# Feed-forward rows prepared in steps behind each output tile; the output stage's products in a written order; the last tile's turns behind the first feed-forward products

## The chip, the core and the metric

The kernel runs on one core of one Trainium2 chip. The core has a matrix engine (TensorE, PE in the profile, with its weight loads listed as PEld), a vector engine (VectorE, DVE), a scalar engine (ScalarE, ACT), GpSimd (POOL) and a sync engine (SP) that here only issues transfers. Each engine works through its own queue in order; engines wait for one another by semaphores. The metric is the time of one execution on the device in microseconds; the time before is the median of three runs, 2523.09 us (2523.03 to 2525.29).

## The reference

One layer of a streaming encoder for 2048 prompt rows and 8 sequences of 16 sample rows, 17 tiles of 128 rows with D = 1024 columns. The change touches the output projection with its two norms and the start of the feed-forward part:

```python
    mix = jnp.concatenate([o, sc_out.astype(x.dtype)], axis=-1) @ w_o
    x = x + rmsnorm(mix, norm_mix_post)

    h = rmsnorm(x, norm_ffn_pre)
    f = (jax.nn.silu(h @ w_gate) * (h @ w_up)) @ w_down
    x = x + rmsnorm(f, norm_ffn_post)
```

All of it is float32. The kernel gets that precision from products of split operands: each operand is cast to a short form (`h`, by ACT) and the rest of it is kept as a second operand (`l`, by a subtraction on DVE or POOL), and each product is three matmuls: h with h, h with l, l with h.

## The kernel before

The program runs in stages: the mixer (input projection and the two head groups), the **output stage** (`o_tile`, once for each tile t of 0 to 16), the feed-forward products (`gate_up`, three groups of rows with 22 column blocks each), and the down projection. The first two stages leave what the next one reads in DRAM; the feed-forward input goes through DRAM too (`hTd`, one tensor for each of three groups of tiles, 0 to 5, 6 to 11 and 12 to 16).

**One output tile.** `o_load(t)` has SP load two halves of the mixer's output (`mr`, one buffer) and the residual rows (`xo`, two buffers). `mix_split` makes the split operand of each half: ACT casts to `mh`, DVE subtracts to `ml`; each of the two names has three buffers of half a tile. Then PE makes 48 products of 512 columns, 8 blocks of rows of `w_o` by three split terms by two halves of the output, into two PSUM banks (`dbank`, of three buffers, and `tbank`, of two). Behind them comes a chain over several engines: two squares with a sum on ACT; a small sum on DVE, and the reciprocal root by a DVE and a POOL instruction (`rstd`, names `oxm`, `oxr`); two products with the gains on DVE, which scale in the bank; two additions to `xo`; two squares of `xo` on ACT; another small sum and root (`oym`, `oyr`); and `hx`, the normed rows, 1024 columns in one instruction, on DVE. Then comes what I call the **turn** of the tile: eight transposes on PE into two `ftbank` banks, two multiplications on DVE into `ht`, and a store of `ht` to `hTd` by ACT's queue.

**The weights of the output projection** (`woh` and `wol`, eight blocks of rows) are cast and subtracted in the stage itself. Blocks 0 and 1 come from SBUF. Blocks 2 to 7 come by DMA through the two buffers that `xo` uses later, so the load of a block waits until the block two before it has been split.

**Preparation of the first feed-forward group.** Between `o_tile` 0 to 7 (`O_SPLIT` = 8) and the rest, `ffn_load(0)` loads the eight blocks of rows of `hTd` of group 0 (`fh`). `ffn_sums` makes four differences (`ft3`) and four more in place. `ffn_prep` makes seven split operands (`PARTS`) of four blocks each: an ACT cast to `xh` and a subtraction to `xl`, with one block in four of group 0 on POOL; two of the seven parts need a further subtraction each. One part stands ahead of each of the next seven `o_tile`.

**What sets the order.** A scheduler that fills each engine's queue from its own model of readiness; written order is a priority only. So before, products of neighbouring tiles mix on PE, and the turns stand where the scheduler puts them. `tc.issue_after(x)` keeps what is inside it behind instruction x. `tc.manual_schedule(engines={PE})`, used in the mixer before, makes PE keep the written order.

**The start of the feed-forward products.** `ffetch` has weights loaded, combined and split; `gu_start(0, 0)` makes four products of 12 matmuls each, and `gate_up` three more and what follows on ACT, DVE and POOL. The eight PSUM banks are used in turn, three `dbank`, two `tbank`, three `ftbank`.

Of the kernel before, what the change touches and what calls it, by code (L numbers as in the profile page):

```python
# [1 line left out]

# [15 lines left out]
P = 128  # L18
D = 1024
KD = D // P  # L20
# [3 lines left out]
NT = 17  # L24
# [20 lines left out]
O_SPLIT = 8  # L45
NPD, NPT, NPG = 3, 2, 2
NR, NKV, NACC = 3, 2, 3
XKB = 4
# [4 lines left out]
NWE = 4  # L53
# [31 lines left out]
def kernel(  # L85
# [28 lines left out]
    nc = tc.nc  # L114
    V, A, G, T = nc.vector, nc.scalar, nc.gpsimd, nc.tensor
# [44 lines left out]
    with ExitStack() as ph:  # L160
# [856 lines left out]
            nc.sync.dma_start(out=xt, in_=x[t])  # L1017
            return mr, xt

        ahead = []  # L1020

        def o_tile(t):
            mr, xt = ahead.pop() if ahead else o_load(t)
            pss = [psd.tile([P, 512], F32, tag="d", name="dbank"), tbank()]
            for kh in range(2):
                mh, ml = mix_split(mr[kh]) if t else ready_m[kh]
                for j in range(4):
                    k = 4 * kh + j
                    for ci, (m_, w_) in enumerate(((mh, woh), (mh, wol), (ml, woh))):
                        for n in range(2):  # L1030
                            T.matmul(pss[n], m_[:, j, :], w_[k][:, n * 512:(n + 1) * 512],  # L1031
                                     start=(k == 0 and ci == 0), stop=(k == KD - 1 and ci == 2))
            ss = op.tile([P, 4], F32, tag="oss", name="oss", bufs=2)
            for n in range(2):
                A.activation(ojunk, pss[n], AF.Square, accum_out=ss[:, n:n + 1])
            V.tensor_add(ss[:, 0:1], ss[:, 0:1], ss[:, 1:2])
            r = rstd(op, ss[:, 0:1], 1, 1.0 / D, EPS, "ox")
            for n in range(2):
                c = slice(n * 512, (n + 1) * 512)
                V.scalar_tensor_tensor(pss[n], pss[n], r, gpost[:, c], op0=ALU.mult, op1=ALU.mult)  # L1040
                V.tensor_add(xt[:, c], xt[:, c], pss[n])
            nc.scalar.dma_start(out=x2d[t], in_=xt)
            for n in range(2):
                A.activation(ojunk, xt[:, n * 512:(n + 1) * 512], AF.Square, accum_out=ss[:, 2 + n:3 + n])
# [3 lines left out]
            V.tensor_scalar_mul(hx, xt, r)  # L1048
            ht = op.tile([P, KD, P], F32, tag="ht", name="ht") if t else spare[1]
            for n in range(2):  # L1050
                ps = pft.tile([P, 512], F32, tag="t", name="ftbank")
                for q in range(4):
                    k = 4 * n + q
                    T.transpose(ps[:, q * P:(q + 1) * P], hx[:, k * P:(k + 1) * P], ident)
                V.tensor_mul(ht[:, 4 * n:4 * n + 4, :], ps.rearrange("p (k c) -> p k c", k=4),
                             g_ffn[:, 4 * n:4 * n + 4].unsqueeze(2).broadcast_to([P, 4, P]))
            gi, i = FPLACE[t]
            nc.scalar.dma_start(out=hTd[gi][:, :, i * P:(i + 1) * P], in_=ht)

        for t in range(O_SPLIT):  # L1060
            o_tile(t)
        ahead.append(o_load(O_SPLIT))


    nbank = [0]
# [66 lines left out]
    with ExitStack() as ph:  # L1132
# [9 lines left out]
        def blocks(gi, hs, k):  # L1142
            hw = len(FGROUPS[gi]) * P // 2
            return hs[k][:, :hw], hs[k][:, hw:2 * hw], hs[KH + k][:, :hw], hs[KH + k][:, hw:2 * hw]

        def ffn_sums(gi, hs, fs):
            hw = len(FGROUPS[gi]) * P // 2
            t3, t2 = [], []
            for k in range(KH):
                b11, b12, b21, b22 = blocks(gi, hs, k)  # L1150
                t3.append(fs.tile([P, HW], F32, tag="t3", name="ft3", bufs=KH)[:, :hw])
                V.tensor_sub(t3[k], b22, b12)
                V.tensor_sub(b12, b12, b11)
# [5 lines left out]
            return t3, t2  # L1159

        def ffn_prep(gi, hs, sums):
            hw = len(FGROUPS[gi]) * P // 2
            t3, t2 = sums
            X = {nm: ([], []) for nm in PARTS}
            for nm in PARTS:
                for k in range(KH):
                    b11, b12, b21, b22 = blocks(gi, hs, k)
                    if nm == "T2" and not gi:
                        V.tensor_sub(b12, b22, b12)
                    elif nm == "T4":  # L1170
                        V.tensor_sub(t2[k], b21, t2[k])
# [4 lines left out]
                    (G if k == 0 and not gi else V).tensor_tensor(  # L1176
                        out=l[:, :hw], in0=v, in1=h[:, :hw].bitcast(F32), op=ALU.subtract)
                    X[nm][0].append(h)
                    X[nm][1].append(l)
                yield X  # L1180
# [70 lines left out]
        def gu_start(gi, f, X):  # L1251
            hw = len(FGROUPS[gi]) * P // 2
            g_, f_, W, _ = fpend[0]
            assert (g_, f_) == (gi, f)
            banks = [fbank()[:, :hw] for _ in range(4)]
            for b, w, nm in zip(banks, W, ("B11", "T3", "T1", "T2")):
# [71 lines left out]
        for gi in range(len(FGROUPS)):  # L1328
# [2 lines left out]
            if gi + 1 < len(FGROUPS):  # L1331
                hload, hs = ffn_load(gi + 1, fd), []
            for f in range(NF):
                gate_up(gi, f, hid, gu_start(gi, f, hid))
                if gi + 1 < len(FGROUPS):
                    if 4 <= f < 4 + KD:
                        with tc.issue_after(wl[0].ins):
                            hs.append(next(hload))
                    if f == NF - 6:
                        t3 = ffn_sums(gi + 1, hs, fd)  # L1340
# [233 lines left out]
```

## Time and profile before

| what | value |
|---|---|
| median of three runs | 2523.09 us |
| the profiled execution: time, and span from first to last instruction | 2523.03 us, 2521.2 us |
| DVE, ACT, POOL busy over the span | 1616.9 us (64%), 1059.6 us (42%), 591.8 us (23%) |
| first product of the output stage | at 906.18 us |
| last product of the output stage | at 1114.88 us |
| the two turns behind that | at 1116.67 and 1132.38 us |
| chain that ended last, by engine | PE 77%, DVE 10%, DMA 5%, ACT 3%, issue 3% |

Times in the profile count from the start of the span. A row of the timeline gives start, duration, engine, line and operation, output and inputs, shapes, and in brackets how long the engine had been idle and what ended that. Matmuls overlap: a row of 0.39 us is followed by the next about 0.23 us later.

### The profile page before, as it was taken

The numbers are of one execution on the slowest core, as the hardware profiler recorded it, in microseconds if no ns is written. First come the engines' busy times: TensorE is split into PE (matmuls) and PEld (weight loads), VectorE is DVE, ScalarE is ACT, GpSimd is POOL, SyncE is SP. The second block draws the span as 40 slices with busy tenths as digits, with TensorE's granted clock in tenths as the row PEclk, the third lists the DMA queues.
The fourth block names the chain that finished last, engine by engine and source line by source line (L and its number), as shares of the span: only waits on it lengthen the run. The fifth ranks groups of instructions, "written<-read, shape, count | busy, mean of one in ns | idle before, by whom it ended". The sixth has DMA issues, their size and how long they took to land.

```text
span 2521.2 us, 39375 instructions
## 1 busy us (share of the span) xinstructions
PE 2462.7 (98%) x14366; PEld 2251.4 (89%) x14366; DVE 1616.9 (64%) x3025; ACT 1059.6 (42%) x2355; POOL 591.8 (23%) x663
## 2 busy tenths in 40 slices
PE   8999999999999999999999999999999999999998
PEld 7988888889999988789999999999999987888786
DVE  5966645545666555868878754545555564677698
ACT  5656445445435343534344422223333345333343
POOL 1101011011010001325556400000000045455564
PEclk9999999999999999999999999999999999999999
DMA  7865555556676556668877878878888844343476
GB/s 264 319 209 194 211 193 192 176 181 226 229 239 237 195 187 223 222 229 319 276 262 260 292 245 276 269 247 259 286 275 303 264 142 129 98 124 123 128 225 184
DMA packets 282498, 561.91 MB, mean 223 GB/s; under 512 B 26108, under 2 KB 174784, under 8 KB 265024
## 3 DMA queue, kind: packets, MB, share of 16 engines
q1 hardware_dynamic: 161200, 483.52, 57.2%
q10 hardware_dynamic: 121104, 75.88, 9.7%
q8 instruction: 113, 1.85, 0.3%
q14 instruction: 81, 0.66, 0.1%
HBM read 400.62 MB, written 158.70 MB: 222 GB/s over the span
## 4 chain that ended last, share of the span: by engine, by line
PE 77%; DVE 10%; DMA 5%; ACT 3%; issue 3%; POOL 1%; ACTq 0%; SPq 0%; DVEq 0%; POOLq 0%
PE fbank L1248 31%; PE dbank L298 21%; PE fbank L1406 10%; PE tbank L1031 3%; PE dbank L1031 3%; DVE xr L1424 1%; DVE acc L1365 1%; DVE acc L302 1%; PE gbank L155 1%; PE tbank L343 1%; DMA partd<-pt 1%; DMA xt<-in_x 1%; PE obank L694 1%; PE gbank L749 1%; PE gbank L702 1%
## 5 line engine op out<-in xcount | busy, mean ns | idle before, releaser
L1248 PE MATMUL fbank<-xh,fw 128*128 128x384 f32 (+1 forms) x3696 | 899.5, 326 | 7.9 <-ACT m L1282 3.5
L298 PE MATMUL dbank<-hi,w 128*128 128x384 f32 (+1 forms) x2240 | 673.3, 369 | 9.1 <-ACT w L277 6.3
L1248 PEld LDWEIGHTS fbank<-xh,fw 128*128 128x128 f32 x3696 | 651.9, 188 | 9.8 <-ACT m L1282 4.3
L1248 PE MATMUL fbank<-xl,fw 128*128 128x384 f32 (+1 forms) x1848 | 602.5, 326 | 0.0
L1406 PE MATMUL fbank<-dw,as 128*128 128x512 f32 x1980 | 458.8, 393 | 8.5 <-DVE as L1390 2.5
L298 PEld LDWEIGHTS dbank<-hi,w 128*128 128x128 f32 x2240 | 417.6, 190 | 48.5 <-ACT w L277 6.6
L1406 PEld LDWEIGHTS fbank<-dw,as 128*128 128x128 f32 x1980 | 370.4, 188 | 96.6 <-DVE acc L1365 4.2
L298 PE MATMUL dbank<-lo,w 128*128 128x384 f32 (+1 forms) x1120 | 402.8, 360 | 1.1 <-DVE lo L216 1.1
L1248 PEld LDWEIGHTS fbank<-xl,fw 128*128 128x128 f32 x1848 | 347.4, 188 | 0.0
L1390 POOL TENSOR_TENSOR as<-ar,as 128x256 fp32r<-128x256 f32 (+1 forms) x207 | 187.1, 914 | 276.8 <-ACT as L1387 273.1
L298 PEld LDWEIGHTS dbank<-lo,w 128*128 128x128 f32 x1120 | 213.3, 190 | 18.7 <-DVE lo L216 1.7
L1365 DVE TENSOR_TENSOR acc<-acc,fbank 128x512 f32<-128x512 f32 x248 | 166.2, 682 | 92.8 <-PE fbank L1406 74.8
L1387 ACT CAST as<-ar 128x256 fp32r<-128x256 f32 (+1 forms) x288 | 118.1, 427 | 182.0 <-PE fbank L1406 133.4
L1105 POOL TENSOR_TENSOR dw<-dr,dw 128x512 fp32r<-128x512 f32 x52 | 77.1, 1495 | 484.6 <-ACT dw L1103 484.4
L1223 ACT CAST fw<-rg 128x512 fp32r<-128x512 f32 x124 | 77.4, 624 | 194.6 <-PE fbank L1248 150.0
L302 DVE SCALAR_TENSOR_TENSOR acc<-R,cw,acc 128x384 f32<-128x384 f32 (+2 forms) x180 | 121.7, 678 | 53.1 <-ACT acc L332 44.4
L1295 DVE TENSOR_TENSOR c<-u,fbank 128x384 f32<-128x384 f32 (+1 forms) x66 | 34.9, 528 | 101.1 <-PE fbank L1248 101.1
L1293 ACT ACTIVATE m<-fbank 128x384 f32<-128x384 f32 (+1 forms) x66 | 31.3, 474 | 125.0 <-PE fbank L1248 113.7
L1291 DVE TENSOR_TENSOR m<-m,m 128x384 f32<-128x384 f32 (+1 forms) x44 | 23.1, 526 | 93.3 <-ACT m L1284 93.3
L324 POOL COPY hist<-R 128x3 f32<-128x3 f32 x60 | 18.5, 308 | 255.5 <-ACT R L307 202.0
L1224 POOL TENSOR_TENSOR fw<-rg,fw 128x512 fp32r<-128x512 f32 x44 | 69.7, 1583 | 34.3 <-ACT fw L1223 34.1
L1224 DVE TENSOR_TENSOR fw<-rg,fw 128x512 fp32r<-128x512 f32 x80 | 56.5, 706 | 17.7 <-ACT fw L1223 15.2
(356 smaller groups left out, 3489.3 us busy)
## 6 DMA issues: line engine op xcount, KB each, us to landing
w<-wsplit SPq DMA_DIRECT2D x105, 1024.0 KB, 5.1
fw<-fsplit SPq DMA_DIRECT2D x188, 512.0 KB, 4.7
fsplit<-fw SPq DMA_DIRECT2D x94, 512.0 KB, 4.2
partd<-pt ACTq DMA_DIRECT2D x88, 384.0 KB, 6.9
rg<-in_w_gu SPq DMA_DIRECT2D x62, 512.0 KB, 4.1
wsplit<-w SPq DMA_DIRECT2D x28, 1024.0 KB, 4.9
ar<-partd SPq DMA_DIRECT2D x48, 384.0 KB, 3.2
wr<-in_w_in SPq DMA_DIRECT2D x34, 512.0 KB, 5.9
```

The source lines that it names most:

```text
L298: T.matmul(ps[:, :c], l[:, k, :], r[k][:, :c], start=(k == 0 and r is hi and l is wh), stop=(k == KD - 1 and l is wl))
L302: r = V.scalar_tensor_tensor(acc, raw(d), w[:, d:d + 1], acc, op0=ALU.mult, op1=ALU.add)
L1031: T.matmul(pss[n], m_[:, j, :], w_[k][:, n * 512:(n + 1) * 512], start=(k == 0 and ci == 0), stop=(k == KD - 1 and ci == 2))
L1105: e.tensor_tensor(out=w[:, 1], in0=v, in1=w[:, 0].bitcast(F32), op=ALU.subtract)
L1223: A.copy(w[:, 0], v)
L1224: e.tensor_tensor(out=w[:, 1], in0=v, in1=w[:, 0].bitcast(F32), op=ALU.subtract)
L1248: T.matmul(ps, w_[:, c], b_[k][:, :hw], start=(first and k == 0 and ci == 0), stop=(k == KH - 1 and ci == 2), skip_group_check=not first)
L1295: V.tensor_add(c21, u2, b3)
L1365: V.tensor_add(dst, dst, ps)
L1387: ins = A.copy(a[:, 0, :n], v)
L1390: e.tensor_tensor(out=a[:, 1, :n], in0=v, in1=a[:, 0, :n].bitcast(F32), op=ALU.subtract)
L1406: T.matmul(ps, a[:, x_, q * P:(q + 1) * P], w[:, y_], start=(start and q == 0 and ci == 0), stop=(q == c - 1 and ci == 2), skip_group_chec ...
```

## The change

Six things are done at once:

1. `o_tile` is cut into `o_products` (the 48 products) and `o_post` (the chain); the turn becomes a function that `o_post` returns, and `o_products` of the next tile calls it behind its first 30 products (second half, `j == 1`).
2. The whole output stage is in a region of manual order on PE.
3. `hx` is made by ACT (a copy with a scale) where it was DVE.
4. `ffn_sums` and `ffn_prep` are generators that yield after each block of four; behind `o_tile` 7 to 15 four steps are taken, inside `issue_after` of that tile's last addition (`omark["V"]`) and last square of the banks (`omark["A"]`). All subtractions of `ffn_prep` are DVE's now. `O_SPLIT` is 7.
5. `o_load(t + 1)` is written behind `o_post(t)`.
6. The last tile's turn is written behind `gu_start(0, 0)`, whose third and fourth bank change places.

```diff
+        def o_products(t, mr, turn):
             pss = [psd.tile([P, 512], F32, tag="d", name="dbank"), tbank()]
             for kh in range(2):
                 mh, ml = mix_split(mr[kh]) if t else ready_m[kh]
                 for j in range(4):
+                    if kh and j == 1 and turn:
+                        turn()
                     k = 4 * kh + j
...
-            V.tensor_scalar_mul(hx, xt, r)
...
+            A.activation(hx, xt, AF.Copy, scale=r)
+
+            def turn():
...
+        region = ExitStack()
+        region.enter_context(tc.manual_schedule(engines={mybir.EngineType.PE}))
+        state_o = {"next": o_load(0), "turn": None}
+
+        def o_tile(t):
+            mr, xt = state_o["next"]
+            pss = o_products(t, mr, state_o["turn"])
+            state_o["turn"] = o_post(t, pss, xt)
+            if t + 1 < NT:
+                state_o["next"] = o_load(t + 1)
...
-                    (G if k == 0 and not gi else V).tensor_tensor(
-                        out=l[:, :hw], in0=v, in1=h[:, :hw].bitcast(F32), op=ALU.subtract)
+                    V.tensor_tensor(out=l[:, :hw], in0=v, in1=h[:, :hw].bitcast(F32), op=ALU.subtract)
...
-            prep = ffn_prep(0, hs, ffn_sums(0, hs, fs))
-            for t in range(O_SPLIT, O_SPLIT + len(PARTS)):
-                hid = next(prep)
+            sums = ffn_sums(0, hs, fs)
+            prep = itertools.chain(sums, ffn_prep(0, hs, next(sums)))
+            for t in range(O_SPLIT, NT - 1):
                 o_tile(t)
+                with tc.issue_after(omark["V"].ins), tc.issue_after(omark["A"].ins):
+                    for hid in itertools.islice(prep, 4):
+                        pass
...
-        for t in range(O_SPLIT + len(PARTS), NT):
-            if t == NT - 1:
-                ffetch(NWE)
-            o_tile(t)
+        ffetch(NWE)
+        o_tile(NT - 1)
+        started = gu_start(0, 0, hid)
+        state_o["turn"]()
+        region.close()
```

How that moves instructions shows in the queues.

**PE, the turn of tile 4.** Rows are matmuls, output and inputs by name; the number behind a name tells buffers apart. Before, `hx_9853` is tile 4 and `dbank_9973` is tile 6:

```order
L1031 MATMUL dbank_9973<-wol1_9342,mh_9975 128x512
L1031 MATMUL tbank_9974<-wol1_9342,mh_9975 128x512
L1054 MATMUL ftbank_9856<-cst_172,hx_9853 128x128 x4
L1054 MATMUL ftbank_9862<-cst_172,hx_9853 128x128 x4
L1031 MATMUL dbank_9973<-woh1_9341,ml_9976 128x512
```

In the change `hx_9855` is tile 4 and `dbank_9862` is tile 5:

```order
L1031 MATMUL dbank_9862<-woh4_9335,ml_9893 128x512
L1031 MATMUL tbank_9863<-woh4_9335,ml_9893 128x512
L1059 MATMUL ftbank_9903<-cst_172,hx_9855 128x128 x4
L1059 MATMUL ftbank_9909<-cst_172,hx_9855 128x128 x4
L1031 MATMUL dbank_9862<-woh5_9333,mh_9892 128x512
```

The turn of tile 4 stood behind all 48 products of tile 5 and ten of tile 6, 58 products behind its own tile's last; now it stands behind 30 products of tile 5. So stand all turns but the last.

**PE, the first two tiles.** Here `dbank_9390` is tile 0 and `dbank_9478` tile 1 before; `woh3` and `woh4` are blocks 3 and 4 of the weights. Before, behind the first half of tile 0:

```order
L1031 MATMUL dbank_9390<-wol3_9338,mh_9349 128x512
L1031 MATMUL tbank_9391<-wol3_9338,mh_9349 128x512
L1031 MATMUL dbank_9390<-woh3_9337,ml_9350 128x512
L1031 MATMUL tbank_9391<-woh3_9337,ml_9350 128x512
L1031 MATMUL dbank_9478<-woh0_9343,mh_9480 128x512
L1031 MATMUL tbank_9479<-woh0_9343,mh_9480 128x512
```

In the change (`dbank_9392` is tile 0):

```order
L1031 MATMUL dbank_9392<-wol3_9338,mh_9349 128x512
L1031 MATMUL tbank_9393<-wol3_9338,mh_9349 128x512
L1031 MATMUL dbank_9392<-woh3_9337,ml_9350 128x512
L1031 MATMUL tbank_9393<-woh3_9337,ml_9350 128x512
L1031 MATMUL dbank_9392<-woh4_9335,mh_9357 128x512
L1031 MATMUL tbank_9393<-woh4_9335,mh_9357 128x512
```

The first half of tile 1, which needs blocks 0 to 3 alone, stood between the halves of tile 0; now the second half of tile 0, with blocks 4 to 7, follows its first half at once. The loads of the blocks stand in SP's queue as before.

**ACT and DVE, the chain of a tile.** ACT in the change, tile 4 (`dbank_9763`; `mr_9956` holds tile 6):

```order
L987 COPY mh_9963<-mr_9956 128x512
L1038 ACTIVATE ojunk_9325,oss_9835<-dbank_9763 128x512
L1038 ACTIVATE ojunk_9325,oss_9835<-tbank_9764 128x512
L1047 ACTIVATE ojunk_9325,oss_9835<-xo_9761 128x512
L987 COPY mh_9991<-mr_9956 128x512
L1045 DMA x2d4_159<-xo_9761 128x1024
L1047 ACTIVATE ojunk_9325,oss_9835<-xo_9761 128x512
L1051 ACTIVATE hx_9855<-xo_9761,oyr_9853 128x1024
```

and DVE in the change, tile 8 (`dbank_10196`), with the first part of the feed-forward rows:

```order
L1043 TENSOR_SCALAR tbank_10197<-tbank_10197,oxr_10274,gpost_9324 128x512
L1044 TENSOR_TENSOR xo_10182<-xo_10182,dbank_10196 128x512
L1044 TENSOR_TENSOR xo_10182<-xo_10182,tbank_10197 128x512
L1195 TENSOR_TENSOR xl_10296<-fh_10069,xh_10295 128x384
L1195 TENSOR_TENSOR xl_10300<-fh_10071,xh_10299 128x384
L1195 TENSOR_TENSOR xl_10304<-fh_10073,xh_10303 128x384
L1195 TENSOR_TENSOR xl_10308<-fh_10075,xh_10307 128x384
L988 TENSOR_TENSOR ml_10457<-mr_10405,mh_10456 128x512
L1048 TENSOR_TENSOR oss_10268<-oss_10268 128x1
L148 TENSOR_SCALAR oym_10284<-oss_10268 128x1
```

On ACT, the cast of the second half of the tile after next (`mh_9991`, into the buffer that the first half of the next tile is read from) stands inside the chain, ahead of its second square of `xo`, and `hx` is ACT's. On DVE, four instructions of the preparation and the `ml` of that cast stand inside the chain, between the last addition and the small sum; in the parts with a further subtraction (tiles 11 and 13) three of the four `xl` stand behind the small sum as well, ahead of `oym`, and behind tile 7 all eight differences stand ahead of `oym`.

More of the change, by code (lines that the diff above doesn't have):

```diff
@@ L1 @@
+import itertools
 from contextlib import ExitStack
@@ L44 @@
 TLS = True
-O_SPLIT = 8
+O_SPLIT = 7
 NPD, NPT, NPG = 3, 2, 2
@@ L1047, in o_tile @@
             hx = op.tile([P, D], F32, tag="hx", name="hx") if t else spare[0]
[L1048 to L1058, printed above, removed]
+            A.activation(hx, xt, AF.Copy, scale=r)
+            def turn():
+                ht = op.tile([P, KD, P], F32, tag="ht", name="ht") if t else spare[1]
+                for n in range(2):
+                    ps = pft.tile([P, 512], F32, tag="t", name="ftbank")
+                    for q in range(4):
+                        k = 4 * n + q
+                        T.transpose(ps[:, q * P:(q + 1) * P], hx[:, k * P:(k + 1) * P], ident)
+                    V.tensor_mul(ht[:, 4 * n:4 * n + 4, :], ps.rearrange("p (k c) -> p k c", k=4),
+                                 g_ffn[:, 4 * n:4 * n + 4].unsqueeze(2).broadcast_to([P, 4, P]))
+                gi, i = FPLACE[t]
+                nc.scalar.dma_start(out=hTd[gi][:, :, i * P:(i + 1) * P], in_=ht)
+            return turn
+        omark = {}
+        region = ExitStack()
[7 more added lines that the diff above has]
+                state_o["next"] = o_load(t + 1)
         for t in range(O_SPLIT):
             o_tile(t)
-        ahead.append(o_load(O_SPLIT))
     nbank = [0]
@@ L1149, in ffn_sums @@
             for k in range(KH):
+                if not gi:
+                    yield t3, t2
                 b11, b12, b21, b22 = blocks(gi, hs, k)
@@ L1255, in gu_start @@
             banks = [fbank()[:, :hw] for _ in range(4)]
+            if not (gi or f):
+                banks = banks[:2] + banks[:1:-1]
             for b, w, nm in zip(banks, W, ("B11", "T3", "T1", "T2")):
@@ L1339 @@
                     if f == NF - 6:
-                        t3 = ffn_sums(gi + 1, hs, fd)
+                        t3 = next(ffn_sums(gi + 1, hs, fd))
                 elif f == 10:
```

15 lines of the change are left out of this document (7 added, 8 removed).

## The prediction

> **What bounds the kernel now.** I read the page's first section, then a table by stage, then who waits for whom around the change. The page's line of the engines comes first; in the table a row is a stretch with its length and the busy time of each engine, the granted clock, the share of the DMA engines and GB/s.
>
> ```profile
> PE 2462.7 (98%) x14366; PEld 2251.4 (89%) x14366; DVE 1616.9 (64%) x3025; ACT 1059.6 (42%) x2355; POOL 591.8 (23%) x663
> ```
> ```profile
> 906.00:912.00 6.00, 5.33 (x21) 3.73 (x22) 5.65 (x9) 4.21 (x7) 0.00 (x0) 1.00 0.89 261
> 912.00:926.00 14.00, 14.00 (x63) 11.61 (x62) 6.89 (x7) 5.45 (x6) 0.00 (x0) 1.00 0.64 214
> 926.00:1020.00 94.00, 94.00 (x444) 78.45 (x443) 59.93 (x117) 40.70 (x103) 14.76 (x21) 1.00 0.64 208
> 1020.00:1041.00 21.00, 15.03 (x57) 11.50 (x57) 18.86 (x40) 8.38 (x20) 8.01 (x6) 0.84 0.45 146
> 1041.00:1115.00 74.00, 74.00 (x356) 61.88 (x355) 46.38 (x92) 26.49 (x67) 10.37 (x15) 1.00 0.66 218
> ```
> ```profile
> PE dbank L1031 <- DVE xo L1041: 4.4, 1, 4.4
> PE ftbank L1054 <- DVE hx L1048: 2.9, 2, 1.6
> PE fbank L1248 <- DVE ht L1055: 2.0, 1, 2.0
> ```
>
> PE bounds it. In the output stage PE stands still only at its start and in 1020 to 1041 us, where the preparation of the feed-forward rows fills DVE (18.86 of 21 us): 4.4 us for a bank that DVE has not emptied and 1.6 of the 2.9 us for `hx`. The other 1.3 us for `hx` and the 2.0 us for `ht` are the last turn, in the first feed-forward products. That is all that the change can win back, together with the clock behind the longest wait:
>
> ```profile
> 1035.50 0.76 PE L1031 MATMUL dbank<-woh,mh 128*128 128x512 f32 x1 [4.36 <-DVE xo L1041]
> ...
> 1040.75 0.41 PE L1031 MATMUL tbank<-woh,mh 128*128 128x512 f32 x1
> ```
>
> Twelve matmuls take 5.25 us, 0.44 each. A tile at full clock is seen from one turn to the next in a quiet part:
>
> ```profile
> 978.60 1.04 PE L1054 MATMUL ftbank<-cst,hx 128*128 128x128 f32 x8
> 979.39 0.48 PE L1031 MATMUL dbank<-woh,ml 128*128 128x512 f32 x1
> 979.70 0.40 PE L1031 MATMUL tbank<-woh,ml 128*128 128x512 f32 x1
> ...
> 990.38 1.04 PE L1054 MATMUL ftbank<-cst,hx 128*128 128x128 f32 x8
> ```
>
> 11.78 us hold 48 products and one turn. The turn costs 0.79 us and a slow first matmul (0.31 where 0.23 is usual), 0.88 together, so a product is (11.78 - 0.88) / 48 = 0.227 us. The twelve slow ones lost 12 x 0.21 = 2.5 us. **What can be won**: 1.6 + 4.4 + 2.5 + 1.3 + 2.0 = 11.8 us.
>
> **Tile 0 in written order.** Its second half needs blocks 4 to 7 of the weights. The last of them:
>
> ```profile
> 923.20 1.05 ACT L1000 CAST woh<-wor 128x1024 fp32r<-128x1024 f32 x1 [1.14 <-DMA wor<-in_w_o]
> ```
> ```profile
> 924.28 1.23 DVE L1001 TENSOR_TENSOR wol<-wor,woh 128x1024 fp32r<-128x1024 f32 x1 [0.97 <-ACT woh L1000]
> ```
>
> The load ends this wait, and SP's queue and the split ahead of it are as before, so block 7 is ready at 925.5 again. Four products of tile 0 follow it: its end is 925.5 + 4 x 0.227 = 926.4. By 926.0 PE had issued 21 + 63 = 84 products before; tile 0's end is the 48th. 36 products are late, 36 x 0.227 = **8.2 us**. Below this it can hardly go (the load sets it); a half clock on these last products would add 1 to 3.
>
> **The turn behind 30 products.** This is the step that decides. It comes due 30 x 0.227 = 6.8 us after the tile's own last product. Is `hx` there by then? The chain of a tile of before, whose successor's first product is the first row (T = 964.54):
>
> ```profile
> 964.54 0.39 PE L1031 MATMUL dbank<-woh,mh 128*128 128x512 f32 x1
> ```
> ```profile
> 964.41 0.62 ACT L986 CAST mh<-mr 128x512 fp32r<-128x512 f32 x1 [4.50 <-DMA mr<-mixo]
> 964.93 0.59 ACT L1035 ACTIVATE ojunk<-dbank 128x512 bf16<-128x512 f32 x1
> ...
> 971.23 0.63 ACT L1044 ACTIVATE ojunk<-xo 128x512 bf16<-128x512 f32 x1
> ...
> 971.98 0.63 ACT L1044 ACTIVATE ojunk<-xo 128x512 bf16<-128x512 f32 x1
> ```
> ```profile
> 967.45 0.76 DVE L1040 SCALAR_TENSOR_TENSOR dbank<-dbank,oxr,gpost 128x512 f32<-128x512 f32 x1 [0.73 <-POOL oxr L149]
> 968.11 0.68 DVE L1055 TENSOR_TENSOR ht<-ftbank,vec 128x512 f32<-128x512 f32 x1
> 968.71 0.75 DVE L1040 SCALAR_TENSOR_TENSOR tbank<-tbank,oxr,gpost 128x512 f32<-128x512 f32 x1
> ...
> 969.97 0.68 DVE L1041 TENSOR_TENSOR xo<-xo,dbank 128x512 f32<-128x512 f32 x1
> 970.56 0.68 DVE L1041 TENSOR_TENSOR xo<-xo,tbank 128x512 f32<-128x512 f32 x1
> ...
> 973.81 0.75 DVE L1048 TENSOR_SCALAR hx<-xo,oyr 128x1024 f32<-128x1024 f32 x1 [0.73 <-POOL oyr L149]
> ```
>
> The squares begin 0.4 behind T, after the cast. DVE's first product with the gain is at T + 2.9. Two such (0.66 each), an addition (0.60) and the last one's 0.68 end at T + 5.5; the two `ht` that stand between them here, 0.60 each, are over before in the change. The second square of `xo` would start there, but ACT's queue has the cast of `mh` ahead of it. Its buffer is read until the 22nd product of the next tile, 21 x 0.227 + 0.39 = T + 5.2, and ACT is in the first square (0.75) from T + 4.95 to 5.7. So cast at 5.7, 0.52 for it (964.41 to 964.93), square at T + 6.2. From that square to `hx` are 1.83 us (971.98 to 973.81): T + 8.05. `hx` on ACT takes what ACT takes for 1024 columns, 1.05 us by the cast of `woh` above; with 0.1 to PE, the transposes start at T + 9.2. PE waits 9.2 - 6.8 = **2.4 us**, in every tile, because it can't take a later product ahead of the turn. The least the rows allow is 5.55 + 1.83 + 1.15 - 6.8 = 1.7, with the cast out of the way. I take 2.4: the queue has the cast there.
>
> Where the preparation lies in the chain, its DVE instructions count too:
>
> ```profile
> 1017.41 0.54 DVE L1176 TENSOR_TENSOR xl<-fh,xh 128x384 fp32r<-128x384 f32 x1
> 1017.88 0.54 DVE L1153 TENSOR_TENSOR fh<-fh 128x384 f32<-128x384 f32 x1
> ```
>
> 0.47 each. DVE, free at T + 5.4, ends four of them at 7.3 and `ml` (0.6) at 7.9, so the small sum comes 1.0 later than the 6.9 without them. The waits behind the tiles:
>
> - 0 to 6: 7 x 2.4 = 16.8
> - 8, 9, 10, 12, 14, four `xl` in the chain: 5 x 3.4 = 17.0
> - 11 and 13, four differences there and three `xl` ahead of `oym` (1.4 more): 2 x 4.8 = 9.6
> - 7, eight differences ahead of `oym`, 8 x 0.47 with `ml`, less the 0.9 that was slack: 5.3
> - 15, no later tile's cast: 1.6
>
> Together **50.3 us**, where before the turn stood 58 products (13.2 us) behind its tile and waited for nothing. The casts of `xh` run on ACT in its pause between the squares; the subtractions that leave POOL shorten no wait here. Bounds: 1.7 each, the preparation hidden, is 27; half a us more in each is 58.
>
> **The clock.** A third cost hangs on these waits. The last three columns of the following rows are the granted clock, the DMA share and GB/s; I cut the stretches where the clock changes, and at whole multiples of their 3.41 us from there.
>
> ```profile
> 1279.70:1283.10 3.40, 1.51 (x9) 1.19 (x8) 0.94 (x2) 1.62 (x4) 0.49 (x1) 1.00 0.96 319
> 1283.10:1286.50 3.40, 3.40 (x13) 3.40 (x12) 3.37 (x4) 1.93 (x4) 3.40 (x3) 0.50 0.96 331
> 1136.30:1139.70 3.40, 2.01 (x12) 1.69 (x10) 3.40 (x4) 1.26 (x3) 2.82 (x2) 1.00 0.99 387
> ```
>
> 1.9 us without work inside one stretch (1.51 busy) were followed by one at half clock; a stretch with 2.01 busy was not. So a wait of about 2.2 us idle halves the clock when most of it lies in one stretch, about two times in three, a wait of 3 or more nearly always. Half a stretch is 1.7 us of PE; what of it falls on the first 30 products of the next tile is hidden, since the turn waits for `hx` anyway. I take 5 full costs in 16 waits, **8.5 us**; ends 0 and 16 x 1.7 = 27. The Trainium skill (TensorE: Matmul & The Clock Gate, "HAM oscillation — how this bites in real kernels") has a milder rule, no idle gaps over about 3.4 us; by it only the three longest waits cost, and the sum would be 3 x 1.7 = 5.1 in place of 8.5, the time 2575 us. The row at 1279.70 speaks against it.
>
> **The feed-forward start.** The last turn behind some 17 us of feed-forward products finds `hx` ready, which gives back 3.3 us, already in the 11.8. Weights may be late there, since DVE has their splits beside the last chain; between -1 and +4, taken as 0. The queues from the sixth column block on are as before.
>
> **Sum.** 8.2 + 50.3 + 8.5 - 11.8 = +55.2 on the profiled execution's 2523.03 us (span 2521.2): 2578 us, and as much against the median, 2523.09.
>
> **Rivals.**
> - The waits without any half clock: 2578 - 8.5 = 2570. For it: most waits are short and can lie across two stretches; against it the row at 1279.70. Chance 0.15.
> - The chain is shorter than I count, waits of 1.7 with the preparation in DVE's pauses: 8.2 + 27 - 11.8 = +23, 2547, with some clock 2555. For it: DVE does pause 1.8 us for the root; against it the order of the queue. Chance 0.12.
> - Everything late: 58 of waits, half clock in ten of them (17), weights late (4): 8.2 + 58 + 17 + 4 - 11.8 = +75, 2598. Chance 0.15.
> - The other side: the turn finds its `hx` there and PE never waits. This decides from a chain of 6.8 us on; then 8.2 - 11.8 gives -3.6, 2519.5, and if block 7 came earlier as well, 2511. Against it: the squares, roots and `hx` alone, with nothing between, sum to 8.5 us by the rows. Chance 0.04.
> - My forecast: 0.54, with 2563 to 2590 as its own range.
>
> **How the numbers follow.** Predicted 2578 us. 2550 to 2596 leaves out the other side, a part of the shorter chain and of the late case, about 2 in 10. Changes under 0.2% (5 us) can't be told from none here: slower 0.96; the other side splits into 0.02 within that and 0.02 faster.
>
> **What would show it.** In the profile after: the turns 14 us apart in tiles 1 to 7 and 15 to 16.5 in 8 to 15; PE idle for ACT's `hx` ahead of the first transpose, 16 times, 2 to 5 us; the cast of `mh` between the two squares of `xo`; tile 0's last product at 926; the last product of tile 16 between 1160 and 1178; stretches of half clock behind the waits. Wrong is the argument if the transposes wait for nothing, if `hx` ends within 7 us of the bank's last product, or if the time is under 2540.

## The result and the profile after

| | before | after |
|---|---|---|
| median | 2523.06 us (4 runs, 2521.03 to 2525.29) | 2595.31 us (4 runs, 2593.4 to 2600.16) |
| profiled execution, span | 2523.03, 2521.2 | 2593.4, 2591.6 |
| first and last product of the output stage | 906.18, 1114.88 | 903.98, 1181.96 |
| start of the 588th feed-forward product (seven column blocks of 84) | 1223.21 | 1290.62 |

The ratio is 1.0285, with a 95% interval of 1.0272 to 1.0298: slower by 72 us. The prediction was 2578 us, range 2550 to 2596, on the side "slower": the measured time lies 0.7 us inside the upper end of that range, and above the forecast's own 2563 to 2590.

The output stage is the first thing to look at. The table by stage, cut at the stage's first and last product, has one row of each kernel (us, then busy time of PE, PEld, DVE, ACT, POOL, granted clock, DMA share, GB/s). Before:

```profile
906.20:1115.10 208.90, 202.44 (x936) 167.22 (x937) 137.51 (x261) 85.04 (x201) 33.13 (x41) 0.98 0.64 207
```

After:

```profile
904.00:1182.20 278.20, 224.26 (x945) 179.26 (x946) 129.13 (x254) 100.15 (x217) 20.97 (x34) 0.92 0.49 160
1182.20:1290.80 108.60, 105.14 (x598) 104.19 (x596) 90.75 (x110) 49.37 (x99) 65.28 (x47) 0.98 0.85 302
```

The stage is 69.3 us longer, nearly the whole of the 70.4 between the two profiled executions. Two parts can be read off: PE's idle time grew from 6.5 to 53.9 us, and its busy time by 21.8 us for the same products and one turn more, at a clock of 0.92 in place of 0.98. The first 588 feed-forward products take 108.7 us, against 108.3 before. What PE waited for, from 890 to 1230 us of the kernel after (us in total, times, longest):

```profile
PE ftbank L1059 <- ACT hx L1051: 48.6, 17, 6.6
PE dbank L1031 <- ACT woh L1001: 3.7, 2, 2.1
PE fbank L1269 <- DVE ht L1060: 2.9, 1, 2.9
PE dbank L1031 <- DVE wol L1002: 1.8, 4, 0.5
```

All seventeen turns wait for `hx`. The timeline of PE shows each, here those of tiles 0, 2, 3, 7, 8, 9, 11, 14 and 15:

```profile
933.34 1.45 PE L1059 MATMUL ftbank<-cst,hx 128*128 128x128 f32 x8 [1.95 <-ACT hx L1051]
...
963.12 1.09 PE L1059 MATMUL ftbank<-cst,hx 128*128 128x128 f32 x8 [2.08 <-ACT hx L1051]
977.20 1.09 PE L1059 MATMUL ftbank<-cst,hx 128*128 128x128 f32 x8 [2.08 <-ACT hx L1051]
...
1039.67 1.97 PE L1059 MATMUL ftbank<-cst,hx 128*128 128x128 f32 x8 [6.58 <-ACT hx L1051]
1056.42 1.65 PE L1059 MATMUL ftbank<-cst,hx 128*128 128x128 f32 x8 [3.09 <-ACT hx L1051]
1073.15 1.32 PE L1059 MATMUL ftbank<-cst,hx 128*128 128x128 f32 x8 [3.10 <-ACT hx L1051]
...
1108.04 1.97 PE L1059 MATMUL ftbank<-cst,hx 128*128 128x128 f32 x8 [4.56 <-ACT hx L1051]
...
1160.86 1.10 PE L1059 MATMUL ftbank<-cst,hx 128*128 128x128 f32 x8 [3.09 <-ACT hx L1051]
1175.52 1.29 PE L1059 MATMUL ftbank<-cst,hx 128*128 128x128 f32 x8 [2.65 <-ACT hx L1051]
```

The idle times of the sixteen turns inside the stage sum to 48.3 us. Idle time is counted from the end of the last product, 0.39 us behind its start, where the next would have started after 0.23: 0.16 more is lost at each wait, 16 x 0.16 = 2.5, so 50.8.

The busy time is the other part. From one plain turn to the next (tiles 0 to 6) it is 14.1 us in most cases (963.12 to 977.20), and 15.7 where a stretch of half clock follows the turn (977.20 to 992.9). Stretches of 3.41 us, two and two, the first with the wait and the second behind it:

```profile
974.89:978.30 3.41, 1.33 (x11) 1.10 (x10) 0.75 (x4) 1.15 (x2) 0.55 (x1) 1.00 0.85 264
978.30:981.72 3.42, 3.42 (x9) 2.67 (x9) 0.88 (x2) 0.00 (x0) 0.00 (x0) 0.50 0.74 250
1053.40:1056.81 3.41, 0.39 (x3) 0.39 (x4) 1.06 (x4) 1.15 (x1) 0.55 (x1) 1.00 0.56 172
1056.81:1060.22 3.41, 3.41 (x13) 2.93 (x12) 1.38 (x2) 0.00 (x0) 0.00 (x0) 0.50 0.75 208
```

In 974.89 to 978.30 PE worked 1.33 us, and 978.30 to 981.72 ran at half clock; the same for 0.39 and the next stretch. Ten of the sixteen distances from a turn to the next (for tile 15, to the end of the stage) are longer than the waits explain, nine by 1.6 us and one by 2.8 (two stretches, from 1142.1): **17.4 us**. The expectations below, written earlier, have 17.8 for it.

### The profile page after: what moved, and what is told of

The parts are those of the page before. It is cut to its first block, busy times and chain, and to the rows that moved or that the text cites. A ratio compares the mean times of both kernels' runs of the same rounds, so it can differ in the third digit from the quotient of the medians.

```text
span 2591.6 us, 39353 instructions
## 1 busy us (share of the span) xinstructions
PE 2483.7 (96%) x14366; PEld 2262.9 (87%) x14366; DVE 1605.3 (62%) x3015; ACT 1074.8 (41%) x2372; POOL 577.4 (22%) x656
## 5 line engine op out<-in xcount | busy, mean ns | idle before, releaser
L299 PEld LDWEIGHTS dbank<-hi,w 128*128 128x128 f32 x2240 | 416.4, 189 | 48.6 <-ACT w L278 6.4
L299 PEld LDWEIGHTS dbank<-lo,w 128*128 128x128 f32 x1120 | 212.6, 190 | 18.6 <-DVE lo L217 1.6
L1059 PE MATMUL ftbank<-cst,hx 128*128 128x128 f32 x136 | 23.1, 325 | 48.6 <-ACT hx L1051 48.6
```

Of the source, the lines that this page charges most:

```text
L299: T.matmul(ps[:, :c], l[:, k, :], r[k][:, :c], start=(k == 0 and r is hi and l is wh), stop=(k == KD - 1 and l is wl))
```

## Experiments

Each kernel differs from the one after the change only by what its diff shows, unless another is named. "Before" was run with each group on the same chip, 2521.8 to 2524.6 us, and the ratios are to that; differences between kernels of different groups are good to 3 us or so. The tiles are counted from 0.

**e2_j3: the turn 12 products later.**

```diff
-                    if kh and j == 1 and turn:
+                    if kh and j == 3 and turn:
```

> The turn stands 12 products later in the next tile, behind 42 in place of 30: 12 x 0.227 = 2.7 us less wait in each. From the idle times of the changed kernel (1.95, six of 2.08, 6.58, five of 3.09, two of 4.55, 2.65) 9.6 of 48.3 us stay, that is 3.9 behind tile 7, 1.8 behind tiles 11 and 13 and 0.4 behind the five others with preparation. Theory (half clock comes with idle time over some 1.7 us in one stretch): about three stretches stay of 10.7, so 2595.3 - 38.7 - 2 (the start of the turn, 0.16 in 13 tiles) - 12.8 = about 2542 us, 2536 to 2548. Rival (the half clock comes with the turn and not with the length of the wait): 2554 to 2557.

Measured: 2543.68 us, ratio to before 1.0073 (1.0049 to 1.0097). The waits for `hx` fell from 48.6 to 13.0 us, in the tiles named but for one: tile 15 waits 2.64 as it did, because in the shorter stage more work on the feed-forward weights falls into its chain (on DVE its small sum stands behind five such instructions, at 1122.82). Four stretches of half clock are left behind turns. The theory's 2542 holds and the rival's 2554 does not; 51.6 us hang on where the turn stands.

**e3_fill: work in the wait.** This one adds nine products ahead of each turn but the last; the transposes overwrite their results.

```diff
                     ps = pft.tile([P, 512], F32, tag="t", name="ftbank")
+                    for _ in range(9 if n == 0 and t < NT - 1 else 0):
+                        T.matmul(ps, woh[0][:, :P], woh[0][:, :512], start=True, stop=True)
```

> Nine products of 512 columns, whose results the transposes overwrite, are added ahead of each of the first 16 turns: 2.04 us of work in the bank of the turn, which needs no hx. Theory (the half clock comes from idle time, and costs 17.8 us in the changed kernel): PE is busy where it waited, only the three long waits keep a half clock (3 x 1.7 = 5), the turns stay where hx puts them: 2595.3 - 17.8 + 5 = about 2582 us, 2577 to 2586, with idle time ahead of the transposes near 0 in tiles 0 to 6 and 1.0 in most others. Rival one (the clock's share was counted right at 8.5): 2588 to 2590. Rival two (the half clock doesn't follow idle time): 2595. Rival three (hx isn't what the turn waits for): nine products more in 16 tiles, 16 x 2.04 = 33 us, 2628.

Measured: 2584.31 us, 1.0228 (1.0207 to 1.0249). PE does 16 x 9 = 144 products more and the kernel is 11 us faster. Turns of tiles 8, 9, 10 and 11 with the fill:

```profile
1055.51 1.09 PE L1061 MATMUL ftbank<-cst,hx 128*128 128x128 f32 x8 [1.06 <-ACT hx L1051]
1070.60 1.09 PE L1061 MATMUL ftbank<-cst,hx 128*128 128x128 f32 x8 [1.05 <-ACT hx L1051]
1085.70 1.09 PE L1061 MATMUL ftbank<-cst,hx 128*128 128x128 f32 x8 [1.06 <-ACT hx L1051]
1102.27 1.09 PE L1061 MATMUL ftbank<-cst,hx 128*128 128x128 f32 x8 [2.51 <-ACT hx L1051]
```

The turns of tiles 8 and 9 stand 15.09 us apart, where they were 16.73 apart: `hx` sets them, and the 1.64 between is half clock alone. The stage took 263.5 us in place of 278.0, so 14.5 of the 17.4 us went with the idle time; of the half-clock stretches behind turns one pair, behind tile 7, is left (the waits of 2.51 us in tiles 11 and 13, which the theory took as still paid, lie across two stretches). That the half clock follows idle time and what it costs is shown.

**e4_tile01: tiles 0 and 1 share the weights.**

```diff
+        def o_first():
+            pss = [[psd.tile([P, 512], F32, tag="d", name="dbank"), tbank()] for _ in range(2)]
...
+            for i in range(2):
+                for j in range(4):
+                    o_step(pss[i], 0, j, *m[i][0])
+            m[1].append(mix_split(mr[1]))
+            for j in range(4):
+                for i in range(2):
+                    o_step(pss[i], 1, j, *m[i][1])
...
```

> Tiles 0 and 1 share the weights block by block as they land: tile 1's first half stands behind tile 0's, and in the second half the two tiles take turns at each block; the turns of tiles 0 and 1 come 36 and 54 products behind their tiles, the others as in the changed kernel. Theory (36 products are late because tile 0 waits for weights alone): 8.2 us less, one wait of a turn (2.2) and its clock less too: 2583 to 2588. Rival (the written order of tile 0 costs nothing, since the turns' chain would stand there anyway): 2593 to 2597.

Measured: 2589.77 us, 1.0253 (1.0231 to 1.0275); 5.5 us less, between theory and rival, and the interval, 5.5 us to each side, excludes neither. The trace shows more: the weights' waits are gone (0.3 us left), and two others came:

```profile
932.97 0.79 PE L1056 MATMUL tbank<-woh,mh 128*128 128x512 f32 x1 [4.23 <-DVE xo L1069]
...
957.38 1.97 PE L1084 MATMUL ftbank<-cst,hx 128*128 128x128 f32 x8 [3.47 <-ACT hx L1076]
```

Tiles 0 and 1 now end together, so tile 2 asks for a `tbank` (there are two) that DVE has not emptied.

**e5_lag8: the turn 60 products behind its tile.**

```diff
-O_SPLIT = 7
+O_SPLIT = 8
...
-                    if kh and j == 1 and turn:
+                    if not kh and j == 2 and turn:
...
+            late_turn = state_o["turns"].pop(0) if len(state_o["turns"]) > 1 else None
+            pss = o_products(t, mr, late_turn)
+            state_o["turns"].append(o_post(t, pss, xt))
...
```

With `O_SPLIT` left at 7 (e1_lag) there is no time: the load of the first group's rows is then written ahead of tile 7, and the turn of tile 5, which stores the last of them, stands in tile 7.

> The turn of tile t-2 stands behind 12 products of tile t, 60 products (13.6 us) behind its own tile's end; the last two turns stand in the first feed-forward products, and the preparation begins one tile later (tile 8), four pieces a tile in 8 to 15, so that its rows are there. Theory (the turn behind 30 products is too early for its hx, and nothing else is): the 16 waits and the half clock behind them go, 2595.3 - 50.8 - 17.8 = about 2527 us, 2520 to 2532, with the turns 11.8 to 12 us apart. Rival one (DVE or ACT has become the bound of the stage, so that hx is late wherever the turn stands): over 2555. Rival two (the written order of the products itself costs it): about 2595, the turns 14 us apart.

Measured: 2544.56 us, 1.0086 (1.007 to 1.0102), 18 above the theory (12 in the profiled execution, the fastest of the four) and under both rivals. In the stage the theory holds for most tiles, with turns 11.8 us apart, but the stage takes 217.3 us where 278.0 - 50.8 - 17.4 = 209.8 was to be expected. Two new waits took what the theory had left out, one in tile 8 and one in the feed-forward start. Around the turn of tile 8, on ACT, SP and PE:

```profile
1038.35 0.62 ACT L987 CAST mh<-mr 128x512 fp32r<-128x512 f32 x1 [6.02 <-DMA mr<-mixo]
...
1039.46 1.14 ACT L1051 ACTIVATE hx<-xo,oyr 128x1024 f32<-128x1024 f32 x1
```
```profile
1033.39 0.32 SPq L1014 DMA_DIRECT2D mr<-mixo  x1
```
```profile
1040.65 1.97 PE L1059 MATMUL ftbank<-cst,hx 128*128 128x128 f32 x8 [4.51 <-ACT hx L1051]
...
1124.36 0.45 PE L1270 MATMUL fbank<-xh,fw 128*128 128x384 f32 x1 [2.12 <-ACT fw L1245]
```

`hx` is not behind its own chain there but behind a cast in ACT's queue, whose `mr` came late: its load was issued at 1033.39, when DVE, behind four differences, had made the last `ml` from the one buffer of `mr` (1032.68 to 1033.3). And the first feed-forward products wait for their weights: their loads go out only at 1119.4, behind the last preparation in tile 15, whose memory they take.

**e6_best: e5_lag8 with tiles 0 to 2 in the order of the weights.** As e4_tile01, and tile 2 makes all products of one bank ahead of the other's.

> The kernel with the late turns, and tiles 0 to 2 in an order that follows the weights: tile 1's first half behind tile 0's, in the second half tiles 0 and 1 by turns at each block, tile 2 one bank after the other, so that its second bank is asked for 24 products later. Theory (the 8.2 us of tile 0 are work that was free to be done there, and the wait for a bank that the earlier run with two tiles by turns showed comes from asking for two banks at once): 8 us under the kernel with the late turns, 2516 to 2521, and no wait for a bank. Rival (the time goes to another wait in tiles 1 to 3, as 4.2 us of it did in the earlier run): equal to the kernel with the late turns or up to 3 us under it.

Measured: 2535.57 us, 1.0056 (1.0041 to 1.0071): 9.0 us under e5_lag8, and no wait for a bank over 0.4 us. In the profiles the stage is 6.6 us shorter, with a new wait of 1.57 us for `hx` in it (the turn of tile 1). So the written order of tile 0 costs its 8 us.

**e7_prep: the preparation behind hx.**

```diff
+            omark["H"] = A.activation(hx, xt, AF.Copy, scale=r)
...
-                with tc.issue_after(omark["V"].ins), tc.issue_after(omark["A"].ins):
+                with tc.issue_after(omark["H"].ins):
```

> The four pieces of preparation of a tile are released by its hx instead of by the last addition and the square before it, so they stand behind the chain on DVE and ACT; turns as in the changed kernel. Theory (the pieces in the chain make the waits of tiles 7 to 14 longer than those of 0 to 6): all waits near 2.1, that is 5 x 1.0 + 2 x 2.5 + 4.5 = 14.5 us less idle time, and of the nine half-clock stretches there about three stay: 2595.3 - 14.5 - 10 = about 2571 us, 2564 to 2578. Rival (the preparation comes late for the feed-forward products instead, or the pieces collide with the next chain): no less than 2588.

Measured: 2580.01 us, 1.0234 (1.0217 to 1.0251), above the range given. The waits of tiles 7 to 14 are 2.06 to 2.08 us each, as the theory has it. But tile 6 waits 4.81 and tile 15 4.94. On DVE at tile 6, the queue has the first difference ahead of `oym` in the order that the scheduler wrote, and it waits for a load:

```profile
1022.91 0.56 DVE L1171 TENSOR_TENSOR ft<-fh 128x384 f32<-128x384 f32 x1 [2.05 <-DMA fh<-hTd]
1023.38 0.15 DVE L148 TENSOR_SCALAR oym<-oss 128x1 f32<-128x1 f32 x1
```

In tile 15 the splits of the feed-forward weights have come into the chain, as in e2_j3. The part that was in doubt, what the pieces cost in the chain, is shown; the sum isn't, for a late load and an early one.

**e8_clear: that, and the cast of mh behind hx.**

```diff
-                mh, ml = mix_split(mr[kh]) if t else ready_m[kh]
+                with tc.issue_after(omark["H"][t - 2].ins) if t > 1 and not kh else ExitStack():
+                    mh, ml = mix_split(mr[kh]) if t else ready_m[kh]
...
```

> As the run before it, and the cast of mh two tiles ahead is released by hx as well, so that it no longer stands between the two squares of xo. Theory (the cast costs the chain 0.65 in each tile): idle time ahead of the turns about 1.4 each, 16 x 1.4 = 23 in place of 48.3 us; at 1.4 hardly a half clock is left, one to three in place of 10.7: 2595.3 - 25 - 14.5 = about 2556 us, 2550 to 2562. Rival one (the square waits for something else, so the cast filled a pause): equal to the run before it. Rival two (the cast is late for its products then): a wait for mh or ml ahead of each tile's first product, 2575 or more.

Measured: 2570.28 us, 1.0192 (1.0176 to 1.0207): 9.7 under e7_prep, 14 above the theory. The plain waits are shorter by 0.45, not 0.65:

```profile
1061.83 1.09 PE L1060 MATMUL ftbank<-cst,hx 128*128 128x128 f32 x8 [1.63 <-ACT hx L1052]
1075.47 1.09 PE L1060 MATMUL ftbank<-cst,hx 128*128 128x128 f32 x8 [1.63 <-ACT hx L1052]
```

Tiles 7 and 15 wait 5.83 and 5.45 us, 8 of the 14, for the two reasons of e7_prep. In tile 7 the first difference waits for its load at the head of DVE's queue, and the turn of tile 6 and the small sum of tile 7 (1026.10) stand behind it:

```profile
1019.82 0.56 DVE L1172 TENSOR_TENSOR ft<-fh 128x384 f32<-128x384 f32 x1 [6.36 <-DMA fh<-hTd]
```

In tile 15 weight splits stand in the chain. None of the fourteen waits of 1.45 to 1.77 us is followed by a half clock.

**e9_steps: e6_best with the preparation in other steps.** Pieces of 2, 2, 6, 6, 6, 6, 4 in tiles 8 to 14, and the turn of tile 15 at the end of tile 16.

```diff
-                    for hid in itertools.islice(prep, 4):
+                    for hid in itertools.islice(prep, STEPS[t]):
...
+            if t == NT - 1:
+                state_o["turns"].pop(0)()
...
```

> The kernel with the late turns and tiles 0 to 2 in the order of the weights, with two edits: the preparation in pieces of 2, 2, 6, 6, 6, 6, 4 in tiles 8 to 14 (four each in 8 to 15 before), and the turn of tile 15 at the end of tile 16's products, so that only the last turn stands in the first feed-forward products. Theory (what is left there is two waits: in tile 8 the four times two differences hold back ml on DVE, and through it the load of mr, the cast of mh and hx, 4.6 us and a half clock of 3.4; and the feed-forward weights are loaded only when the last piece has left its buffers, in tile 15 of the run before, 7 us): 2535.6 - 8 - 7 = about 2520 us, 2516 to 2526, with no wait over 1 us for hx ahead of tile 15's turn. Rival (the feed-forward start is bound by DVE's and ACT's work on the weights beside the last chain, wherever the preparation ends): 2527 to 2530.

Measured: 2527.47 us, 1.0013 (1.0004 to 1.0022), 8.1 under e6_best (10 when each is set against "before" on its own chip), where 15 were expected. The time is the rival's, the reason is not: the weights' first load now goes out at 1099.7, no product waits for weights, and the first 588 feed-forward products take 109.8 us where they took 115.7. It is the stage that gave back only 2.1 us (208.7 after 210.8). Six turns wait for `hx`, 10.1 us together. Five of them are in the stage, 0.92 to 1.79 us each, where the theory had none over 1; in tile 9 the first square on ACT stands behind a cast whose load is late, as in e5_lag8:

```profile
1032.45 0.62 ACT L988 CAST mh<-mr 128x512 fp32r<-128x512 f32 x1 [2.75 <-DMA mr<-mixo]
```

The longest is the turn of tile 15, which stands 48 products behind its tile, with its `hx` behind weight casts and a square of tile 16 in ACT's queue:

```profile
1115.40 0.60 ACT L1075 ACTIVATE ojunk<-dbank 128x512 bf16<-128x512 f32 x1
...
1115.98 0.61 ACT L1281 CAST fw<-rg 128x512 fp32r<-128x512 f32 x1
1116.49 0.62 ACT L1281 CAST fw<-ru 128x512 fp32r<-128x512 f32 x1
1117.01 0.62 ACT L1281 CAST fw<-sD 128x512 fp32r<-128x512 f32 x1
1117.53 1.15 ACT L1088 ACTIVATE hx<-xo,oyr 128x1024 f32<-128x1024 f32 x1
```
```profile
1118.73 1.65 PE L1096 MATMUL ftbank<-cst,hx 128*128 128x128 f32 x8 [3.31 <-ACT hx L1088]
```

**e10_mid: the turns later once more.** As e9_steps; the turn stands behind 24 products of the tile two further on, and that of tile 15 between the second and the third feed-forward product.

```diff
-                    if not kh and j == 2:
+                    if kh and j == 0:
                         state_o["turns"].pop(0)()
...
-            if t == NT - 1:
-                state_o["turns"].pop(0)()
...
+                if nm == "T1" and not (gi or f):
+                    state_o["turns"].pop(0)()
                 product(b, w, X[nm], True)
```

> The run before it, with the turn of tile t-2 behind 24 products of tile t in place of 12, and the turn of tile 15 between the second and the third of the first feed-forward products in place of the end of tile 16. Theory (in the run before, six turns still waited 10.1 us for hx, the longest 3.3 with a half clock of 1.7, since hx was up to 3.3 us late; 12 products are 2.7 us, and ACT's weight casts lie ahead of tile 15's hx only up to 1118): the waits go, 2527.5 - 10.1 - 1.7 = about 2516 us, 2513 to 2521, under the kernel before the change by 3 to 10. Rival (the hx of a tile waits for the turn of the tile ahead, which frees its buffer, so later turns make later hx: the wait moves on with the turn): 2524 to 2530.

Measured: **2514.51 us, 0.9965 (0.9952 to 0.9979)**, faster than the kernel before the change by 9 us, and by 81 than the one after it. Its table by stage, from a profiled execution that was the slowest of its five (2519.89):

```profile
906.90:1108.10 201.20, 200.15 (x936) 165.19 (x937) 124.00 (x252) 99.46 (x216) 20.58 (x34) 1.00 0.64 208
1108.10:1218.40 110.30, 106.42 (x605) 105.04 (x604) 91.14 (x113) 51.43 (x100) 65.79 (x49) 0.98 0.93 331
```

and all that turns wait for `hx` in it:

```profile
PE ftbank L1094 <- ACT hx L1086: 0.2, 1, 0.2
```

The stage has PE idle for 1.05 us of 201.2, at full clock, 7.7 us shorter than before. The rival (a later turn makes a later `hx`) is out.

## Why the prediction was right, and where it was wrong

**Direction and mechanism** were right: PE keeps the written order, so it waits in every tile for an `hx` that lets the transposes start 9.0 us behind the tile's end, while the turn comes due after 6.8. The chain of tile 3 after the change, with the first product of tile 4 and then on ACT:

```profile
968.16 0.39 PE L1031 MATMUL dbank<-woh,mh 128*128 128x512 f32 x1
```
```profile
968.43 0.59 ACT L1038 ACTIVATE ojunk<-dbank 128x512 bf16<-128x512 f32 x1
...
973.03 0.63 ACT L1047 ACTIVATE ojunk<-xo 128x512 bf16<-128x512 f32 x1 [3.21 <-issue]
...
973.66 0.60 ACT L987 CAST mh<-mr 128x512 fp32r<-128x512 f32 x1
974.17 0.63 ACT L1047 ACTIVATE ojunk<-xo 128x512 bf16<-128x512 f32 x1
...
976.00 1.15 ACT L1051 ACTIVATE hx<-xo,oyr 128x1024 f32<-128x1024 f32 x1 [1.11 <-POOL oyr L150]
```

With T = 968.16, the first product of the next tile as in the prediction, the second square of `xo` stands at T + 6.0 (predicted 6.2), behind the cast of `mh`, `hx` at T + 7.8 (8.05), and the transposes at 977.20, T + 9.0 (9.2).

Term by term, in us:

| term | predicted | measured |
|---|---|---|
| tile 0 in written order | +8.2 | +8.3 (its last product starts 20.2 us behind the stage's first; the kernel before had started between 84 and 85 by then); 9.0 by e6_best against e5_lag8 |
| waits for `hx`, sixteen turns | +50.3 | +50.8 |
| half clock behind them | +8.5 | **+17.4** |
| old stalls of the stage | -8.5 | -8.5 |
| one turn more inside the stage (sixteen in place of fifteen) | 0 | +0.9 |
| feed-forward start, with one turn fewer | -3.3 | **+0.3** |
| start of the stage, and everything behind the first 588 feed-forward products | 0 | -2.2 and +3.0 |
| sum | +55.2 | +70.0 of 70.4 |

In the first term the prediction's 84 products by 926.0 count one twice, which lies across 912.00; that is 0.2 us. The waits came out well in their kinds too; with the 0.16 of the slow start they are 2.2 in plain tiles (2.4 predicted), 3.25 with four pieces (3.4), 4.7 in tiles 11 and 13 (4.8), 6.7 in tile 7 (5.3) and 2.8 in tile 15 (1.6). In tile 7 the cause given is there, the eight differences stand ahead of `oym` on DVE. What the prediction left out is a late load: ACT's queue has the cast of `mh` ahead of the tile's first square, and it starts only at 1027.61, 1.5 us behind the first product of tile 8 (1026.12), where the cast in the chain of tile 3 starts 0.3 ahead of that point:

```profile
1027.61 0.62 ACT L987 CAST mh<-mr 128x512 fp32r<-128x512 f32 x1 [6.59 <-DMA mr<-mixo]
```
```profile
1033.17 1.96 DVE L1171 TENSOR_TENSOR ft<-fh 128x384 f32<-128x384 f32 x4
...
1037.60 0.15 DVE L148 TENSOR_SCALAR oym<-oss 128x1 f32<-128x1 f32 x1
```

In tile 15 work on the feed-forward weights stands ahead of the small sum on DVE, which starts at 1168.40, 2.5 us behind the first product of tile 16 (1.7 in tile 3).

**The clock was mis-sized.** The step that failed is "I take 5 full costs in 16 waits". It took one wait in three as fully paid, because half-clock products among the first 30 of a tile were to be hidden by the next wait. But the half-clock stretch begins within about 1 us of the turn, and the 18 products behind the turn are the last of the tile in work: what is lost on them moves that tile's end, its chain and all that follows, and nothing hides it. Of the nine waits of 2.6 us and more, eight were paid for (1160.86 was not); of the seven of about 2 us, two (four of fourteen in e7_prep), where the prediction had two times in three. So fewer waits halved the clock than these shares give, ten of sixteen, and all ten were paid. The distance between turns also matters: 16.73 us in the tiles with preparation is near five stretches (17.07), so that the half-clock stretches begin at 1056.8, 1073.9, 1090.9, 1108.0, 1125.1 and 1142.1, each time within 1.1 us of a turn, with the wait in the stretch just ahead. That this nearness keeps every wait paid is what the rows suggest; no run changed the distance alone. On the Trainium skill's rule (TensorE: Matmul & The Clock Gate, "HAM oscillation — how this bites in real kernels"), no idle gaps over about 3.4 us, the runs decide against it: waits of 1.95, 2.08 and 2.65 us were followed by half clock.

**The feed-forward start** gave nothing back. The last turn did stand 17.5 us behind the stage, and `hx` was late by 0.33 all the same. Then the products waited for a bank:

```profile
1199.66 1.09 PE L1059 MATMUL ftbank<-cst,hx 128*128 128x128 f32 x8 [0.33 <-ACT hx L1051]
...
1209.56 0.44 PE L1269 MATMUL fbank<-xh,fw 128*128 128x384 f32 x1 [2.95 <-DVE ht L1060]
```

DVE took `ht` only at 1208.83, behind the splits of the next weights and the sums of the first column block in its queue, and the wait halved the clock from 1210.4. The prediction had "weights may be late" there; late was the work behind the transposes. The 3.0 us behind the first 588 products come in code that the change does not touch; one half-clock stretch more (at 1981.8) is about half of it, and the rest stays open.

The rivals: "the turn finds its hx" needed a chain of 6.8 us and met 9.0. "Everything late", 2598, comes nearest in time, through its clock (17) and a feed-forward start that gave nothing back; its waits of 58 did not come. "No half clock" is out by e3_fill, "shorter chain" by the 50.8 us of waits.

That 2595 lies in the range, by 0.7 us, is in part luck: the clock (+8.9), the feed-forward start (+3.6) and the code behind it (+3.0) all went the same way, and one of the four executions, 2600.16, lies above the range. Of the signs given in advance the waits, the cast between the squares and the half clock came; the waits reached 6.6 us (2 to 5 given), the turns of the later tiles stood up to 18.6 us apart (15 to 16.5), and the last product of tile 16 started at 1181.96 (1160 to 1178).

## What to carry to other kernels

Where an engine's order is written by hand, put an instruction with a long chain ahead of it as far back as the longest chain with everything that shares its queues, not as far as the chain alone; here 30 products were 2 to 7 us too few, 60 left five waits and 48 in tile 15 a sixth (e9_steps), and 72 were enough. Price a repeated wait twice: its length, and the half clock behind it, in full where the slowed work is on the path to the next wait. Once the first wait goes, look at once for the next one in the queues (a cast behind a late load, a weight split ahead of a small sum); four kernels (e5, e6, e9, e10) led from the first late turn to a stage with 1 us of idle time.

## What the runs showed of the hardware

A wait far shorter than a stretch of 3.41 us can halve the clock for the next stretch: stretches in which PE was busy for 1.33 us (shown above) and 1.51 (the prediction's row at 1279.70) did, one with 1.53 (the first row below) did not, so no sharp bound is seen. The eleven traces narrow it: with stretches of 3.41 us laid at the changes of the clock from 880 to 2450 us, all 59 at full clock with up to 1.45 us of busy PE were followed by half clock, 14 of 41 with 1.46 to 1.76, and none of 4878 with more. The fourteen waits of 1.45 to 1.77 us in e8_clear left at least 1.64 us of work in their stretches and were never followed by one; the fourteen waits of 1.96 to 2.08 us in e7_prep were in four cases, with 1.34 to 1.45 us of work in the stretch.

```profile
961.24:964.65 3.41, 1.53 (x11) 1.45 (x12) 0.84 (x2) 1.15 (x1) 0.55 (x1) 1.00 0.80 220
...
1206.99:1210.41 3.42, 0.85 (x5) 0.85 (x6) 3.42 (x6) 0.48 (x1) 0.29 (x1) 1.00 1.04 386
1210.41:1213.82 3.41, 3.41 (x12) 3.41 (x11) 0.85 (x2) 1.10 (x2) 0.04 (x1) 0.50 1.05 388
```

So filling the waits with products that nobody reads made the kernel faster, by 11 us, although `hx` came no earlier behind its tile (e3_fill).
